# Joining the two token parts behind one stationary weight tile in the column products of a four-layer trunk

## Chip, core and metric

The kernel runs on one core of a Trainium2 chip. The metric is the device time of one execution in microseconds (us). Before the change three runs gave 1311.87 to 1312.33 us, with a median of 1312.16 us. Engines are named as in the profile: PE is the matrix engine (PEld is its loading of stationary operands), DVE the vector engine, ACT the scalar engine, POOL the general one, SP the one that issues most DMAs.

## What is computed

A trunk of four layers over 256 tokens of width 1024. Each layer has a mixer (differential attention, a gated recurrence called hgrn2, windowed attention called swa, differential attention again), a feed-forward network and a gate. Cut to its frame, the reference is:

```python
for i in range(DEPTH):
    y = (diff_attention, hgrn2, swa_sink_attention)[i % 3](h, ...)
    h = layer_norm(ALPHA * h + y, ln_g[i, 0], ln_b[i, 0])
    u = jnp.square(jax.nn.relu(h @ w_up[i])) @ w_down[i]      # 1024 -> 4096 -> 1024
    h = layer_norm(ALPHA * h + u, ln_g[i, 1], ln_b[i, 1])
    h = h + jax.nn.sigmoid(h @ w_ple_gate[i]) * (p[i] @ w_ple[i])
```

All of it is float32. The matrix products with weights are the bulk of the work.

## The kernel before

**Split products.** Each float32 operand of a product with weights is split into a high and a low float32r part: ACT copies the high part, DVE subtracts it from the source (`split`, L116 and L117). A product is then three matmuls, high with high, high with low, low with high, into one accumulator (`mm3`, L169 to L171). The weights of the whole trunk are packed on the host into chunks of 128 x 2048 numbers, read in the order of use (`read_w`), three raw buffers deep, and split into tiles `wh` and `wl`, of which four chunks are held.

**Two forms.** In the token-major form (`tokmm`) the tokens are stationary and 512 columns of weights move. In the column form (`colmm`, called by `col2`) a 128 x 128 tile of weights is stationary and 256 tokens move, so that the result comes out with its columns on the partitions. `col2` computes two such column tiles, `c` = 0 and 1, into the two halves of one PSUM bank: for each, eight k-tiles of 128 rows, three matmuls each. Then it calls `done(bank)`. The tokens' two parts are the tiles `hTh` and `hTl`, 128 x 8 x 256 each.

**Where the column form is used.** One chunk for each call of `col2`: 55 chunks of the up projection (`up` in `ffn`), 16 for query and key of the heads in the two differential attentions (`qk_gen`), 8 for query and forget gate in hgrn2 (`qf_gen`), 5 for key, value and query in swa (`kv_done`, `q_gen`). That is 84 chunks and 84 x 16 = 1344 pairs of a column tile and a k-tile, so 4032 matmuls of 256 columns. The `done` functions empty the bank: a Relu on ACT in `up` (L418) and a square on DVE (L419), copies on ACT in the attentions (L607, L611, L782), a sigmoid on ACT and two DVE operations in hgrn2 (L965 to L969).

**Order.** Dense products are generators in one queue (`push`), and the mixers pull them between the steps of their own work with `fill(us)`: each step of a generator yields an estimate of its time, 0.325 for a k-tile of `colmm`. In the feed-forward network the up product of chunk j + 1 comes ahead of the down product of chunk j, which accumulates in four banks called `acc`; the column form and all others use four banks called `mm`. ACT and DVE keep the order that the scheduler gave them and work on splits of later weights between the evictions.

Of the kernel before, what the change touches and what calls it, by code (L numbers as in the profile page):

```python
# [16 lines left out]
P = 128  # L17
D = 1024
S = 256
# [13 lines left out]
# chunks of weights that may be split ahead of earlier work on the scalar engine, and of  # L33
# softmax and relu work on the vector engine
# [7 lines left out]
def backward(ap):  # L42
    """The same view with its last dimension read from the end."""
    dims = [list(d) for d in ap.ap]
    step, n = dims[-1]
    dims[-1] = [-step, n]
    return bass.AP(ap.tensor, ap.offset + (n - 1) * step, dims)


class Weights:  # L50
    """A chunk of weights, split into two float32r parts, in halves of HC columns."""
# [4 lines left out]
    def sl(self, o, n):  # L56
        h, r = o // HC, o % HC
        return [t[h][:, r : r + n] for t in self.tiles]


class Trunk:
# [58 lines left out]
    # the engine's later splits of weights stay behind what it has been given so far  # L120
# [63 lines left out]
    def colmm(self, out, hT, w, col, width):  # L184
        for kt in range(KT):
            self.mm3(
                out, w.sl(kt * width + col, P), [x[:, kt, :] for x in hT], kt == 0, kt == KT - 1
            )
            yield 0.325

    # two column tiles of 128 into the halves of one bank, then done(bank)
    def col2(self, hT, done):
        w = self.load_w()
        ps = self.mm_ps()
        for c in range(2):
            yield from self.colmm(ps[:, c * S : c * S + S], hT, w, c * P, 256)
        done(ps)

    # token-major projection to 512 columns (4 k-tiles a chunk), then evac(blk, bank)
# [17 lines left out]
    # part c of a 1024 -> 1024 projection of one block (2 k-tiles a chunk)  # L217
# [6 lines left out]
    def new_hT(self):  # L224
        return [
            self.hp.tile([P, KT, S], F32R, name=self.nm(t), tag=t, bufs=2)
            for t in ("hTh", "hTl")
        ]

    def load_x(self, blk, k, pool):  # L230
        # four k-tiles of the transposed input
        xr = pool.tile([P, 4, P], F32, name=self.nm("qk"), tag="qk", bufs=3)
        self.nc.sync.dma_start(xr, self.ins["xT"][blk][:, k : k + 4])
        sl = slice(blk * P, blk * P + P)
        self.split(self.hT[0][:, k : k + 4, sl], self.hT[1][:, k : k + 4, sl], xr)

    def setup(self):
        nc, cp = self.nc, self.cp
        self.hT = self.new_hT()
        # keep the tensor engine busy while the first loads are under way: its clock is  # L240
        # gated to half when idle
        z = self.sp.tile([P, 512], BF16, name="z", tag="z", bufs=1)
# [9 lines left out]
    def bias_rows(self, pool):  # L252
        nc, cp, ins = self.nc, self.cp, self.ins
        # relative position biases, one row per head, by distance
# [26 lines left out]
    def load_bias(self, bt, a, lo, hi):  # L281
        d = self.ud[a]
        # row p holds query 127 - p of a block: the distance falls along the row
        src = bass.AP(d.tensor, d.offset + lo * UL, [[1, P], [UL, hi - lo], [1, 256]])
        self.nc.sync.dma_start(bt[:, lo:hi], src)
# [8 lines left out]
    def rpow(self, out, var, scale, eps):  # L294
        # out = (var * scale + eps) ** -0.5
# [45 lines left out]
    def out_part(self, c, blk):  # L341
        # k-tiles 2c, 2c + 1
# [11 lines left out]
    def out_end(self, i, later):  # L354
        # what is left of block 0, of block 1, then the work that needs neither
# [20 lines left out]
    # per-layer embedding, a generator for each block  # L376
# [26 lines left out]
    def ffn(self, i, last):  # L403
# [3 lines left out]
        with tc.tile_pool(name=f"fp{i}", bufs=4) as fp:  # L407
# [16 lines left out]
            # first chunks token-major, so that block 0 needn't wait for block 1  # L424
# [25 lines left out]
            def up(j):  # L450
                def done(ps):
                    r = relu2(ps, 512)
                    new_u(j)
                    self.split(us[j][0], us[j][1], r.rearrange("p (k t) -> p k t", k=2))

                yield from self.col2(hT, done)

# [58 lines left out]
            # gated per-layer embedding  # L516
# [30 lines left out]
    # the transposes of block 1 come when the next mixer has started on block 0  # L547
# [4 lines left out]
    def diff_attention(self, i):  # L552
# [5 lines left out]
        with tc.tile_pool(name=f"ap{i}", bufs=2) as ap:  # L558
# [45 lines left out]
            def qk_gen(hd):  # L604
                def done(ps):
                    qk = ap.tile([P, 2, S], F32, name=self.nm("qk"), tag="qk", bufs=3)
                    nc.scalar.copy(  # L607
                        qk[:, 0, :].rearrange("p (b t) -> p b t", b=2),
                        backward(ps[:, :S].rearrange("p (b t) -> p b t", b=2)),
                    )  # L610
                    nc.scalar.copy(qk[:, 1, :], ps[:, S:])  # L611
                    qks[hd] = qk
# [141 lines left out]
    def swa(self, i):  # L754
# [3 lines left out]
        with tc.tile_pool(name=f"ap{i}", bufs=2) as ap:  # L758
# [8 lines left out]
            def kv_done(ps):  # L767
                nc.scalar.copy(kv.rearrange("p a t -> p (a t)"), ps)
# [10 lines left out]
            def q_gen(c):  # L779
                def done(ps):  # L780
                    q = ap.tile([P, 2, S], F32, name=self.nm("q"), tag="q", bufs=3)
                    nc.scalar.copy(  # L782
                        q.rearrange("p a (b t) -> p (a b) t", b=2),
                        backward(ps.rearrange("p (n t) -> p n t", n=4)),
                    )
                    for n in range(2):
                        qs[2 * c + n] = q[:, n, :]
# [3 lines left out]
            def soft(a):  # L791
                # heads a (partitions 0..63) and a + 8 (partitions 64..127)
# [100 lines left out]
    def hgrn2(self, i):  # L893
        nc, tc, ins = self.nc, self.tc, self.ins
        with tc.tile_pool(name=f"ap{i}", bufs=2) as ap:
# [12 lines left out]
            # lower bound: softmax over depth, sum of rows 1..i  # L908
# [48 lines left out]
            def qf_gen(pr):  # L957
                qt[pr] = ap.tile([P, 2, S], F32, name=self.nm("hq"), tag="hq")
                Ft[pr] = ap.tile([P, 2, S], F32, name=self.nm("f"), tag="f")
                for a in range(2):  # L960
                    hd = 2 * pr + a

                    def done(ps):
                        sig = ap.tile([P, 512], F32, name=self.nm("sig"), tag="sig")
                        nc.scalar.activation(sig, ps, AF.Sigmoid)  # L965
                        nc.vector.tensor_tensor(
                            qt[pr][:, a, :], sig[:, :S], ps[:, :S], op=ALU.mult
                        )
                        nc.vector.tensor_scalar(  # L969
                            Ft[pr][:, a, :], sig[:, S:], ol[:, hd : hd + 1], lb[:, hd : hd + 1],  # L970
                            op0=ALU.mult, op1=ALU.add,
                        )
# [7 lines left out]
            def decay(pr):  # L980
                q, QP, KS, f = qt.pop(pr), Qt.pop(pr), Kt.pop(pr), Ft.pop(pr)
                # diagonal of the transposed decay products, zeros beside it
# [14 lines left out]
                for lv, h in enumerate(LEVELS):  # L997
                    # the first halves of level 32 and 64 are runs of rows: nothing beside them
# [146 lines left out]
def _cols(w, cols):  # L1145
    # [1024, n] -> [128, 8 * 256], k-tile major, of the given 256 columns
# [3 lines left out]
def _half(w):  # L1150
    # [1024, 512] -> two chunks of 4 k-tiles
# [4 lines left out]
def _rows(w):  # L1156
    # [n * 256, 1024] -> n chunks of 2 k-tiles
# [21 lines left out]
def pack(inputs, depth=DEPTH):  # L1179
# [38 lines left out]
    # distances by position in the reversed bias row: rel = 255 - position  # L1218
# [51 lines left out]
```

## Time and profile before

| what | value |
|---|---|
| median of three runs | 1312.16 us |
| the profiled execution's span, first to last instruction | 1310.3 us |
| median less span | 1.9 us |
| PE busy | 1303.0 us, 8378 matmuls |
| DVE busy | 874.1 us |
| ACT busy | 676.0 us |
| DMA | 240.26 MB, mean 183 GB/s |

The page gives the busy time of each engine and the chain of work that ended last. A busy time of PE counts overlapping matmuls once and does not say at which rate they follow each other; for that the starts of consecutive matmuls are read from the time line. Windows of the trace tell how full DVE is in a given stage.

### The profile page before, as it was taken

To read this page: it belongs to the slowest core of one execution; us is meant where nothing else is said; L and a number is where in the kernel's file an instruction comes from. 1 tells how busy PE (TensorE), PEld (TensorE's weight loads), DVE (VectorE), ACT (ScalarE), POOL (GpSimd) and SP (SyncE) were. 2 spreads that over 40 slices of the span, in tenths; PEclk is the share of its full clock that TensorE was granted. 3 is DMA by queue.
4 is the path that set the end of the run, shared out by engine and by line. 5 is a ranking of instruction groups with operands and counts; after the bars stand their busy time and mean duration, and the time that the engine had idled before them with its cause. 6 is when DMAs were issued, how large, how long until landed. Compare 5 with 4: busy or idle time off the path is not lost.

```text
span 1310.3 us, 21010 instructions
## 1 busy us (share of the span) xinstructions
PE 1303.0 (99%) x8378; PEld 1161.2 (89%) x8378; DVE 874.1 (67%) x1573; ACT 676.0 (52%) x1212; POOL 33.7 (3%) x44
## 2 busy tenths in 40 slices
PE   8999999999999999999999999999999999999998
PEld 6988999998899889999989888999989989999987
DVE  5877655557878876555577796555577777655556
ACT  4875544443743454444437755444446775444433
POOL 0001000000000010000000000000000000000000
PEclk9999999999999999999999999999999999999999
DMA  7845655453742356545547145554538344655540
GB/s 268 316 142 193 226 193 188 179 184 132 261 156 103 105 189 227 176 181 191 193 164 266 62 172 213 206 184 190 193 129 295 130 169 161 239 182 190 194 161 33
DMA packets 43091, 240.26 MB, mean 183 GB/s; under 512 B 4512, under 2 KB 11744, under 8 KB 16496
## 3 DMA queue, kind: packets, MB, share of 16 engines
q1 hardware_dynamic: 42992, 238.91, 50.3%
q8 instruction: 66, 1.08, 0.3%
q14 instruction: 33, 0.27, 0.1%
HBM read 237.79 MB, written 1.10 MB: 182 GB/s over the span
## 4 chain that ended last, share of the span: by engine, by line
PE 98%; DMA 1%; ACT 0%; DVE 0%; SPq 0%; issue 0%
PE mm L169 21%; PE mm L171 21%; PE mm L170 20%; PE acc L171 9%; PE acc L170 9%; PE acc L169 9%; PE acc L1010 2%; PE mm L309 1%; DMA wr<-in_w_dram 1%; PE mm L664 1%; PE acc L628 1%; PE acc L624 1%; DMA qk<-in_xT_dram 0%; PE acc L841 0%; PE mm L441 0%; PE acc L852 0%
## 5 line engine op out<-in xcount | busy, mean ns | idle before, releaser
L117 DVE TENSOR_TENSOR wl<-wr,wh 128x1024 fp32r<-128x1024 f32 (+1 forms) x548 | 511.6, 967 | 248.4 <-ACT wh L116 247.9
L116 ACT ACTIVATE wh<-wr 128x1024 fp32r<-128x1024 f32 (+1 forms) x548 | 443.7, 852 | 366.1 <-issue 141.8
L169 PE MATMUL mm<-hTh,wh 128*128 128x256 f32 x1344 | 384.5, 286 | 0.0
L171 PE MATMUL mm<-hTh,wl 128*128 128x256 f32 x1344 | 380.2, 283 | 0.2 <-DVE wl L117 0.2
L170 PE MATMUL mm<-hTl,wh 128*128 128x256 f32 x1344 | 380.1, 283 | 0.0
L169 PEld LDWEIGHTS mm<-hTh,wh 128*128 128x128 f32 x1344 | 257.0, 191 | 4.4 <-issue 1.8
L170 PEld LDWEIGHTS mm<-hTl,wh 128*128 128x128 f32 x1344 | 257.1, 191 | 2.4
L171 PEld LDWEIGHTS mm<-hTh,wl 128*128 128x128 f32 x1344 | 257.0, 191 | 0.5 <-DVE wl L117 0.4
L169 PE MATMUL acc<-wh,uh 128*128 128x512 f32 x512 | 202.2, 395 | 0.0
L171 PE MATMUL acc<-wh,ul 128*128 128x512 f32 x512 | 202.0, 395 | 0.0
L170 PE MATMUL acc<-wl,uh 128*128 128x512 f32 x512 | 201.8, 394 | 0.0
L169 PE MATMUL mm<-wh,hTh 128*128 128x512 f32 (+1 forms) x536 | 197.2, 368 | 1.4 <-ACT hTh L116 0.7
L170 PE MATMUL mm<-wl,hTh 128*128 128x512 f32 (+1 forms) x536 | 192.8, 360 | 0.5 <-DVE wl L117 0.5
L171 PE MATMUL mm<-wh,hTl 128*128 128x512 f32 (+1 forms) x536 | 192.6, 359 | 0.0
L171 PEld LDWEIGHTS acc<-wh,ul 128*128 128x128 f32 x512 | 96.4, 188 | 22.8
L169 PEld LDWEIGHTS mm<-wh,hTh 128*128 128x128 f32 x536 | 101.4, 189 | 16.2 <-ACT wh L116 1.5
L171 PEld LDWEIGHTS mm<-wh,hTl 128*128 128x128 f32 x536 | 101.2, 189 | 16.0 <-issue 1.0
L170 PEld LDWEIGHTS mm<-wl,hTh 128*128 128x128 f32 x536 | 101.4, 189 | 14.7 <-DVE wl L117 1.5
L169 PEld LDWEIGHTS acc<-wh,uh 128*128 128x128 f32 x512 | 96.7, 189 | 19.9
L170 PEld LDWEIGHTS acc<-wl,uh 128*128 128x128 f32 x512 | 96.5, 188 | 20.0
L116 ACT ACTIVATE uh<-r 128x512 fp32r<-128x512 f32 x55 | 34.8, 632 | 77.0 <-DVE r L419 77.0
L300 POOL TENSOR_TENSOR rs<-rp,mhalf 128x2 f32<-128x2 f32 (+2 forms) x36 | 31.3, 870 | 1234.1 <-DVE rp L299 1234.1
(164 smaller groups left out, 1002.3 us busy)
## 6 DMA issues: line engine op xcount, KB each, us to landing
wr<-in_w_dram SPq DMA_DIRECT2D x207, 1024.0 KB, 4.8
lng<-in_ln_g_dram SPq DMA_DIRECT2D x8, 512.0 KB, 3.8
lnb<-in_ln_b_dram SPq DMA_DIRECT2D x8, 512.0 KB, 4.9
bt<-ud SPq DMA_DIRECT2D x2, 2048.0 KB, 9.9
wr<-in_w_dram SPq DMA_DIRECT2D x8, 256.0 KB, 5.6
bt<-ud SPq DMA_DIRECT2D x1, 1280.0 KB, 14.4
qk<-in_xT_dram SPq DMA_DIRECT2D x4, 256.0 KB, 6.0
h<-in_x_dram SPq DMA_DIRECT2D x2, 512.0 KB, 12.5
```

The costliest lines, as they stand in the source:

```text
L116: self.nc.scalar.activation(hi, src, AF.Copy),
L117: self.nc.vector.tensor_tensor(lo, src, hi.bitcast(F32), op=ALU.subtract),
L169: mm(out, l[0], r[0], start=start, stop=False)
L170: mm(out, l[0], r[1], start=False, stop=False)
L171: mm(out, l[1], r[0], start=False, stop=stop)
L300: nc.gpsimd.tensor_tensor(out, t, self.mhalf[:, :n], op=ALU.pow)
L309: nc.tensor.transpose(pt[:, j * P : j * P + P], src[:, c : c + P], self.ident)
L624: nc.tensor.matmul(sc[:, 0:P], qk[r, 0, 0:P], qk[r, 1, 0:P], start=True, stop=True)
L628: nc.tensor.matmul(sc[:, P:384], qk[r, 0, P:S], qk[r, 1, :], start=True, stop=True)
L664: nc.tensor.transpose(pt[:, s], e[:, 0, s], self.ident)
L1010: nc.tensor.matmul(pl[lo:hi, o : o + w], KS[:, a, b * P + lo : b * P + hi], Qr[:, a, n0 : n0 + g, 1, :], start=True, stop=True,)
```

## The change

The tokens' two parts become one tile of 128 x 8 x 2 x 256, `both`, whose views are the old high and low parts. `colmm` now gives each column tile a whole bank. For each k-tile the high weights meet the 512 columns of both parts in one matmul, and the low weights meet the high part in a second matmul of 256 columns, which adds to the bank's upper half. The two halves are added when the bank is emptied (`join`): ACT copies the upper half to a small tile `cr`, DVE adds the lower half to it. `done` is called for each column tile, not for the two together. The Relu of `up` moves to DVE: one operation computes max(r, 0) times r. hgrn2's sigmoids work on the joined tiles of 256 columns. The estimate of a k-tile becomes 0.35.

```diff
+class Tokens(list):
+    def __init__(self, both):
+        super().__init__([both[:, :, 0, :], both[:, :, 1, :]])
+        self.both = both
...
-    def colmm(self, out, hT, w, col, width):
+    def colmm(self, bank, hT, w, col, width):
+        mm = self.nc.tensor.matmul
         for kt in range(KT):
-            self.mm3(
-                out, w.sl(kt * width + col, P), [x[:, kt, :] for x in hT], kt == 0, kt == KT - 1
-            )
-            yield 0.325
+            wh, wl = w.sl(kt * width + col, P)
+            mm(bank, wh, hT.both[:, kt].rearrange("p a t -> p (a t)"), start=kt == 0, stop=False)
+            mm(bank[:, S:], wl, hT[0][:, kt, :], start=False, stop=kt == KT - 1)
+            yield 0.35
+
+    def join(self, out, bank, rev=False):
+        x = self.wp.tile([P, S], F32, name=self.nm("cr"), tag="cr", bufs=2)
+        self.nc.scalar.copy(x, bank[:, S:])
+        views = [y.rearrange("p (b t) -> p b t", b=2) for y in (out, bank[:, :S], x)]
+        if rev:
+            views[1:] = [backward(y) for y in views[1:]]
+        self.nc.vector.tensor_tensor(*views, op=ALU.add)
...
     def col2(self, hT, done):
         w = self.load_w()
-        ps = self.mm_ps()
         for c in range(2):
-            yield from self.colmm(ps[:, c * S : c * S + S], hT, w, c * P, 256)
-        done(ps)
+            ps = self.mm_ps()
+            yield from self.colmm(ps, hT, w, c * P, 256)
+            done(c, ps)
...
             def up(j):
-                def done(ps):
-                    r = relu2(ps, 512)
-                    new_u(j)
-                    self.split(us[j][0], us[j][1], r.rearrange("p (k t) -> p k t", k=2))
+                r = fp.tile([P, 512], F32, name=self.nm("r"), tag="r", bufs=2)
+
+                def done(c, ps):
+                    self.join(r[:, c * S : c * S + S], ps)
 
                 yield from self.col2(hT, done)
+                nc.vector.scalar_tensor_tensor(r, r, 0.0, r, op0=ALU.max, op1=ALU.mult)
+                new_u(j)
+                self.split(us[j][0], us[j][1], r.rearrange("p (k t) -> p k t", k=2))
...
             def qk_gen(hd):
-                def done(ps):
-                    qk = ap.tile([P, 2, S], F32, name=self.nm("qk"), tag="qk", bufs=3)
-                    nc.scalar.copy(
-                        qk[:, 0, :].rearrange("p (b t) -> p b t", b=2),
-                        backward(ps[:, :S].rearrange("p (b t) -> p b t", b=2)),
-                    )
-                    nc.scalar.copy(qk[:, 1, :], ps[:, S:])
-                    qks[hd] = qk
+                def done(c, ps):
+                    if c == 0:
+                        qks[hd] = ap.tile([P, 2, S], F32, name=self.nm("qk"), tag="qk", bufs=3)
+                    self.join(qks[hd][:, c, :], ps, c == 0)
...
-                    def done(ps):
-                        sig = ap.tile([P, 512], F32, name=self.nm("sig"), tag="sig")
-                        nc.scalar.activation(sig, ps, AF.Sigmoid)
-                        nc.vector.tensor_tensor(
-                            qt[pr][:, a, :], sig[:, :S], ps[:, :S], op=ALU.mult
-                        )
-                        nc.vector.tensor_scalar(
-                            Ft[pr][:, a, :], sig[:, S:], ol[:, hd : hd + 1], lb[:, hd : hd + 1],
-                            op0=ALU.mult, op1=ALU.add,
-                        )
+                    def done(c, ps):
+                        x = ap.tile([P, S], F32, name=self.nm("sig"), tag="sig", bufs=3)
+                        self.join(x, ps)
+                        if c == 0:
+                            y = ap.tile([P, S], F32, name=self.nm("sig"), tag="sig", bufs=3)
+                            nc.scalar.activation(y, x, AF.Sigmoid)
+                            nc.vector.tensor_tensor(qt[pr][:, a, :], x, y, op=ALU.mult)
+                        else:
+                            nc.scalar.activation(x, x, AF.Sigmoid)
+                            nc.vector.tensor_scalar(
+                                Ft[pr][:, a, :], x, ol[:, hd : hd + 1], lb[:, hd : hd + 1],
+                                op0=ALU.mult, op1=ALU.add,
+                            )
```

PE in an up product, first column tile, two k-tiles, before (`mm_...` is the bank, `hTh` and `hTl` the token parts, the last name the stationary weights):

```order
L169 MATMUL mm_2720<-hTh_1374,wh_2712 128x256
L170 MATMUL mm_2720<-hTl_1375,wh_2712 128x256
L171 MATMUL mm_2720<-hTh_1374,wl_2713 128x256
L169 MATMUL mm_2720<-hTh_1374,wh_2716 128x256
L170 MATMUL mm_2720<-hTl_1375,wh_2716 128x256
L171 MATMUL mm_2720<-hTh_1374,wl_2717 128x256
```

and now, the end of a first column tile and the start of the second, which has a bank of its own:

```order
L197 MATMUL mm_2080<-hT_1284,wh_2076 128x512
L198 MATMUL mm_2080<-hT_1284,wl_2077 128x256
L197 MATMUL mm_2100<-hT_1284,wh_2072 128x512
L198 MATMUL mm_2100<-hT_1284,wl_2073 128x256
L197 MATMUL mm_2100<-hT_1284,wh_2072 128x512
L198 MATMUL mm_2100<-hT_1284,wl_2073 128x256
```

Three matmuls of a k-tile became two, with the same 768 columns. DVE in the feed-forward network, from one square to the next, before (`r` is the eviction's tile, `ul` the low part of its split, `wl` the low parts of later weights):

```order
L419 TENSOR_TENSOR r_2469<-r_2469 128x512
L117 TENSOR_TENSOR ul_2473<-r_2469,uh_2472 128x512
L117 TENSOR_TENSOR wl_2679<-wr_2676,wh_2678 128x1024
L117 TENSOR_TENSOR wl_2683<-wr_2676,wh_2682 128x1024
L117 TENSOR_TENSOR wl_2713<-wr_2710,wh_2712 128x1024
L117 TENSOR_TENSOR wl_2717<-wr_2710,wh_2716 128x1024
```

and now:

```order
L125 TENSOR_TENSOR wl_2218<-wr_2215,wh_2217 128x1024
L125 TENSOR_TENSOR wl_2222<-wr_2215,wh_2221 128x1024
L208 TENSOR_TENSOR r_2069<-mm_2080,cr_2097 128x256
L125 TENSOR_TENSOR wl_2253<-wr_2250,wh_2252 128x1024
L125 TENSOR_TENSOR wl_2257<-wr_2250,wh_2256 128x1024
L208 TENSOR_TENSOR r_2069<-mm_2100,cr_2117 128x256
L475 SCALAR_TENSOR_TENSOR r_2069<-r_2069 128x512
L125 TENSOR_TENSOR ul_2122<-r_2069,uh_2121 128x512
```

Two additions of 256 columns are new; the first stands between the splits of two chunks of weights. DVE in hgrn2 ahead of the first pair's decay products, which read `hq` and `KS`, before:

```order
L966 TENSOR_TENSOR hq_3591<-sig_3723,mm_3674 128x256
L969 TENSOR_SCALAR f_3592<-sig_3723,ol_3460,lb_3459 128x256
L117 TENSOR_TENSOR wl_4055<-wr_4046,wh_4054 128x512
L977 TENSOR_SCALAR KS_3728<-f_3592 128x512
L978 TENSOR_TENSOR QP_3727<-hq_3591,f_3592 128x512
```

and now:

```order
L208 TENSOR_TENSOR sig_3451<-mm_3434,cr_3452 128x256
L982 TENSOR_TENSOR hq_3357<-sig_3451,sig_3455 128x256
L125 TENSOR_TENSOR wl_3785<-wr_3782,wh_3784 128x512 x2
L125 TENSOR_TENSOR wl_3791<-wr_3782,wh_3790 128x512
L208 TENSOR_TENSOR sig_3475<-mm_3458,cr_3476 128x256
L125 TENSOR_TENSOR wl_3791<-wr_3782,wh_3790 128x512
L985 TENSOR_SCALAR f_3358<-sig_3475,ol_3227,lb_3226 128x256
L993 TENSOR_SCALAR KS_3482<-f_3358 128x512
```

`KS` now stands behind an addition, a split and the forget gate `f`, whose sigmoid ACT computes after that addition.

## Rows read from the trace of the kernel before

**Rows 1.** The page: PE's busy time, granted clock in 40 slices, chain that ended last.

```profile
PE 1303.0 (99%) x8378; PEld 1161.2 (89%) x8378; DVE 874.1 (67%) x1573; ACT 676.0 (52%) x1212; POOL 33.7 (3%) x44
...
PEclk9999999999999999999999999999999999999999
...
PE 98%; DMA 1%; ACT 0%; DVE 0%; SPq 0%; issue 0%
```

**Rows 2.** PE's waits: waiter, releaser, us in total, times, longest; five in all.

```profile
PE acc L246 <- DVE z L243: 1.2, 1, 1.2
...
PE mm L171 <- DVE wl L117: 0.2, 1, 0.2
```

**Rows 3.** Groups by form: count, busy us, mean ns of one; L170, L171 alike.

```profile
L169 PE MATMUL mm<-hTh,wh 128*128 128x256 f32 x1344 | 384.5, 286 | 0.0
```

**Rows 4.** Time line of PE, an up product: start us, duration us, line; 14 steps apart.

```profile
212.31 0.28 PE L169 MATMUL mm<-hTh,wh 128*128 128x256 f32 x1
...
213.99 0.28 PE L171 MATMUL mm<-hTh,wl 128*128 128x256 f32 x1
```

**Rows 5.** Time line of PE in the first layer's gate: 14 steps apart.

```profile
319.19 0.39 PE L171 MATMUL mm<-wh,hTl 128*128 128x512 f32 x1
...
322.37 0.39 PE L170 MATMUL mm<-wl,hTh 128*128 128x512 f32 x1
```

**Rows 6.** Time line of PE: a down product's first and last matmul, then up.

```profile
205.66 0.39 PE L169 MATMUL acc<-wh,uh 128*128 128x512 f32 x1
...
211.00 0.40 PE L171 MATMUL acc<-wh,ul 128*128 128x512 f32 x1
211.24 0.28 PE L169 MATMUL mm<-hTh,wh 128*128 128x256 f32 x1
211.36 0.28 PE L170 MATMUL mm<-hTl,wh 128*128 128x256 f32 x1
```

**Rows 7.** Time line of PE in mixers: after 512 columns 256; after 256, 512.

```profile
354.53 0.28 PE L169 MATMUL mm<-hTh,wh 128*128 128x256 f32 x1
354.64 0.28 PE L170 MATMUL mm<-hTl,wh 128*128 128x256 f32 x1
...
1054.58 0.40 PE L169 MATMUL mm<-wh,hTh 128*128 128x512 f32 x1
1054.82 0.40 PE L170 MATMUL mm<-wl,hTh 128*128 128x512 f32 x1
```

**Rows 8.** Groups by form: evictions and operations like the new ones.

```profile
L418 ACT ACTIVATE r<-mm 128x512 f32<-128x512 f32 x55 | 31.9, 580 | 9.1 <-PE mm L171 9.1
L328 DVE SCALAR_TENSOR_TENSOR h<-h,mv,lng 128x512 f32<-128x512 f32 x32 | 22.5, 745 | 0.0
L117 DVE TENSOR_TENSOR hTl<-acc,hTh 128x256 fp32r<-128x256 f32 x24 | 10.0, 419 | 1.1 <-ACT hTh L116 0.9
L611 ACT COPY qk<-mm 128x256 f32<-128x256 f32 x16 | 5.9, 367 | 0.0
```

**Rows 9.** Windows: length, busy us of PE, PEld, DVE, ACT, POOL; clock; DMA; GB/s.

```profile
27.00:92.00 65.00, 64.91 (x500) 58.81 (x501) 50.67 (x170) 50.56 (x155) 2.82 (x4) 1.00 0.67 249
140.00:300.00 160.00, 160.00 (x1008) 144.47 (x1007) 91.28 (x93) 72.04 (x84) 0.00 (x0) 1.00 0.54 198
365.00:470.00 105.00, 105.00 (x813) 96.37 (x812) 88.37 (x215) 42.33 (x101) 4.42 (x4) 1.00 0.33 122
370.00:387.00 17.00, 17.00 (x161) 16.62 (x159) 15.30 (x41) 5.58 (x10) 0.00 (x0) 1.00 0.32 122
```

**Rows 10.** Time lines of DVE and PE in hgrn2, ahead of the first decay.

```profile
368.65 0.42 DVE L977 TENSOR_SCALAR KS<-f 128x512 f32<-128x512 f32 x1
...
370.00 0.39 PE L989 MATMUL acc<-hq,KS 128*128 128x128 f32 x2
```

**Rows 11.** Time lines of ACT and PE in the first attention, a head's scores.

```profile
36.08 0.37 ACT L611 COPY qk<-mm 128x256 f32<-128x256 f32 x1
...
37.44 0.38 PE L624 MATMUL acc<-qk 64*128 64x128 f32 x2
```

More of the change, by code (lines that the diff above doesn't have):

```diff
@@ L224, in new_hT @@
     def new_hT(self):
[L225 to L228, printed above, removed]
+        t = self.hp.tile([P, KT, 2, S], F32R, name=self.nm("hT"), tag="hT", bufs=2)
+        return Tokens(t)
     def load_x(self, blk, k, pool):
@@ L239, in setup @@
         self.hT = self.new_hT()
-        z = self.sp.tile([P, 512], BF16, name="z", tag="z", bufs=1)
+        z = self.wp.tile([P, 512], BF16, name="z", tag="cr", bufs=2)
         nc.vector.memset(z, 0.0)
@@ L765, in swa, with kv_done @@
             v = ap.tile([P, 2, P], F32, name=self.nm("v"), tag="v", bufs=1)
-            def kv_done(ps):
-                nc.scalar.copy(kv.rearrange("p a t -> p (a t)"), ps)
+            def kv_done(c, ps):
+                self.join(kv[:, c, :], ps)
             kvg = self.push(self.col2(hT, kv_done))
@@ L779, in q_gen, with done @@
             def q_gen(c):
-                def done(ps):
[L781 to L784, printed above, removed]
-                    )
-                    for n in range(2):
-                        qs[2 * c + n] = q[:, n, :]
+                def done(n, ps):
+                    q = ap.tile([P, S], F32, name=self.nm("q"), tag="q", bufs=6)
+                    self.join(q, ps, True)
+                    qs[2 * c + n] = q
                 return self.push(self.col2(hT, done))
@@ L961, in qf_gen @@
                     hd = 2 * pr + a
-                    def done(ps):
-                        sig = ap.tile([P, 512], F32, name=self.nm("sig"), tag="sig")
-                        nc.scalar.activation(sig, ps, AF.Sigmoid)
-                        nc.vector.tensor_tensor(
-                            qt[pr][:, a, :], sig[:, :S], ps[:, :S], op=ALU.mult
-                        )
-                        nc.vector.tensor_scalar(
-                            Ft[pr][:, a, :], sig[:, S:], ol[:, hd : hd + 1], lb[:, hd : hd + 1],
-                            op0=ALU.mult, op1=ALU.add,
-                        )
+                    def done(c, ps):
[11 more added lines that the diff above has]
+                            )
                     yield from self.col2(hT, done)
```

## The prediction

> **What bounds the kernel now.** I read the page first. PE is busy for 1303.0 of 1310.3 us, the granted clock is at its upper level of 2.4 GHz in all 40 slices, and 98% of the chain that ended last is PE [rows 1]. Then the waits: five rows name PE as the waiter, the longest 1.2 us, the shortest 0.2 us, all at the start of the program [rows 2]. So nothing keeps PE waiting after the first microseconds. The time is the sum of the steps from one matmul's start to the next, and only what shortens these steps, or makes PE wait, shows.
>
> The column form has three groups of 1344 matmuls of 256 columns [rows 3]. The mean of one, 286 ns, is how long one stays in the pipeline, not its price. The price is the step between starts: in an up product 14 steps take 213.99 - 212.31 = 1.68 us, **120 ns** each [rows 4]. At 2.4 GHz 256 columns are 106.7 ns, so 13.3 ns go with the instruction. The kernel also has runs of 512 columns. In the gate 14 steps take 322.37 - 319.19 = 3.18 us, **227 ns** [rows 5], which is 213.3 + 13.7. The two agree: about 13.3 ns for each matmul with its own stationary tile, whatever its width. In the down products the step is longer: 23 steps from 205.66 to 211.00, 232 ns [rows 6].
>
> **PE's part of the change.** Columns stay the same (512 + 256 against 3 x 256), and one instruction of three goes. A pair of column tile and k-tile cost 3 x 120 = 360 ns; it will cost 227 + 120 = 347 ns if the 512 goes at the gate's step. 1344 x 13.3 ns = **17.9 us** less.
>
> No row shows the new mixture, 512 and 256 in turn, so I bound it by the changes of width that exist. Cheap end: the first 256 after a run of 512 steps in 354.64 - 354.53 = 0.11 us [rows 7], and with 227 the pair is 340 ns, 26.9 us less. Dear end: a down product's last 512 takes 0.24 us and the first 256 behind it 0.12 us (211.00, 211.24, 211.36) [rows 6]; read between the two rounded figures and the 360 of now that is about 357 ns, 4 us less. Going from 256 to 512, the first 512 takes 0.24 us [rows 7]: what is gained on one side of a change of width is given back on the other, 240 + 110 = 350. I stay at 347, nearest to the gate's row: the new matmuls write the same `mm` banks, and one operand is a weight tile and the other a token tile, as in the gate, while the 232 ns belong to the `acc` banks and the `u` tiles alone. An up product between two down products runs at 120, like those in the mixers, so it is not the stage that is slow.
>
> For a matmul's step the Trainium skill (TensorE: Matmul & The Clock Gate, section "Back-to-back issue gap") has columns over 2.4 plus 2.5 ns, for matmuls warm and alone. By it one matmul less in each pair is worth 1344 x 2.5 ns = 3.4 us, not 17.9. The rows don't agree with it: their excess is 13.3 ns for either width.
>
> **ACT and DVE.** In `up` ACT had one Relu of 580 ns and now has two copies of 367 ns: +0.15 us a chunk. DVE gains two additions, priced by the like subtraction from PSUM at 419 ns, and its square becomes a fused operation of 745 ns [rows 8]: about +0.9 us a chunk. In the network a chunk of up and one of down take 48 x 0.120 + 24 x 0.232 = 11.3 us, and DVE is busy 91.28 of 160 us there, 57% [rows 9]; 0.9 of 11.3 makes 65%. The cover is PE's own work on a chunk of down products ahead of the use. The first addition waits for half an up product, and two splits of a later chunk are queued behind it; those weights are wanted three or four chunks later, and their buffers come free only late in that same up product. So nothing there reaches PE: cost 0. If the cover were gone, it would be 55 x 0.9 = 50 us.
>
> In the mixers DVE is fuller: 50.67 of 65 us in the first attention, 88.37 of 105 in hgrn2, 15.30 of 17 in the first decay [rows 9]. Three places can make PE wait.
>
> *First decay of hgrn2.* `KS` was ready at 369.07 and used at 370.00, a slack of 0.93 us [rows 10]. The way from bank to `KS` was a sigmoid and DVE operations; now it is copy, addition, sigmoid, gate, `KS`: about 0.37 + 0.42 + 0.37 + 0.42 + 0.42 = 2.0 us and four changes of engine, each of which can find a split of up to 0.7 us at work. Estimate: between 0 and 1 us of wait, taken 0.5.
>
> *Decay products.* Four additions in the first decay are 4 x 0.34 to 0.42 us on 15.30, so about 16.8 us, in a stretch that PE would now pass in 17 - 28 x 0.0133 = 16.6. DVE becomes as long as PE. Splits of later weights can move out of the stretch, so the wait lies between 0 and 1 us, and the second decay is alike; taken 0.5 each.
>
> *Heads of the attentions.* The key copy ended at 36.45 and the scores started at 37.44: 0.99 us, the shortest slack of the 16 heads [rows 11]. The new tail has one copy less behind the last matmul and one addition more, with a hand-over: about +0.3 us, and at worst a split of 0.7 on top. Between 0 and 0.5 us a head, 0 to 8 in all; taken 1. In swa half of the queries are ready half a chunk earlier than before: 0.
>
> Sum of waits: 0.5 + 1 + 1 = 2.5 us, between 0 and about 11. On the profiled execution: 1310.3 - 17.9 + 2.5 = 1294.9 us; its span is 1.9 us under the median, so the **forecast is 1297 us**. DMA (54% busy in the network) need not go faster by more than 1%.
>
> **Rivals.**
> 1. *The dear step in the network.* The 880 up pairs cost 357 ns, since they stand between down products, and the 464 of the mixers 347: 2.6 + 6.2 - 2.5 = 6.3 us less, **1306**. For it: rows 6. Against: the 256s there settle at 120.
> 2. *A 512 behind a 256 stays dear.* Each new 512 stands behind a 256, and the one such step in the mixers took 0.24 us [rows 7], as a down product's last 512 did [rows 6]. Then the pair costs 240 + 120 = 360 ns as before, and the waits are left: 2.5 us more, **1315**, within 0.2%. Against: the steps of rows 5, and that a first 256 behind a 512 gives the same amount back. The skill's figure of 2.5 ns for each matmul leads to the same verdict by another way: 3.4 us less for PE, 2.5 more in waits, 1311.
> 3. *Slower: DVE becomes the bound of the mixers.* 29 chunks there bring 58 additions of 0.42 us, 24.4 us. If all of it came on PE's path, 24.4 - 17.9 = 6.5 us more, **1319**. It decides where DVE's idle time in a stage is less than its additions. Against: 14.3 us idle in the first attention for 16 additions of 6.7 us in all, 16.6 in hgrn2 [rows 9]. For: in-order queues, and the decays at 90%.
> 4. *The cheap step.* 340 ns a pair and 2.5 us of waits: **1288**. Against: the first 512 behind a 256 takes longer than 227 by about as much.
>
> That the change doesn't do what it says is not open: PE's order has 2688 matmuls for the 4032.
>
> **How the numbers follow.** A measurement of this kernel can tell about 0.2%, 2.6 us, from no change. Forecast (1291 to 1303) 0.58; rival 1 0.14; rival 2 0.10; rival 3 0.10; rival 4 0.08. Faster: 0.58 + 0.14 + 0.08 = 0.80. Same: 0.10. Slower: 0.10. The range leaves out rivals 2 and 3: 1287 to 1308.
>
> **What the profile after would show.** Starts of the new matmuls: 227 (512 to 256) and 120 (256 to 512), 347 a pair; 357 or more proves rival 1 or 2, by whether mixers and network differ. An up chunk of 16 pairs: 5.55 us against 5.76. PE's waits after the start: none in the network; waits on `KS`, `QP` and `qk` of some tenths in the mixers, 1 to 5 us in all; over 15 us is rival 3. DVE busy near 874 + 84 x 0.85 = 945 us. I am wrong if the pair steps in over 355 ns, or if PE waits in the network for `r`, `uh` or `wl`.

## The result and the profile after

The changed kernel takes 1302.76 us (median of 4 runs, 1302.48 to 1303.4), the kernel before 1312.06 us (4 runs on the same chip, 1311.87 to 1312.33): a ratio of **0.9931, 95% interval 0.9919 to 0.9943**, 9.3 us less. The forecast was 1297 us, 15 less: the sign and the mechanism are right, two fifths of the gain are missing.

The page after, the rows that answer to [rows 1]: span, busy times, granted clock, chain.

```profile
span 1300.8 us, 18541 instructions
...
PE 1293.9 (99%) x7034; PEld 1087.8 (84%) x7034; DVE 936.8 (72%) x1741; ACT 692.3 (53%) x1296; POOL 35.2 (3%) x44
...
PEclk9999999999999999999999999999999999999999
...
PE 98%; DMA 1%; ACT 0%; DVE 0%; issue 0%; SPq 0%
```

PE has 7034 matmuls for 8378, the clock is at its upper level throughout, and the chain is still PE. Its waits after, all of them, as [rows 2]:

```profile
PE acc L264 <- DVE z L261: 1.2, 1, 1.2
PE mm L177 <- ACT hT L124: 0.5, 1, 0.5
PE acc L177 <- ACT uh L124: 0.4, 1, 0.4
PE mm L177 <- ACT wh L124: 0.2, 1, 0.2
PE mm L178 <- DVE wl L125: 0.2, 1, 0.2
```

Nothing waits for `KS`, `qk` or an addition. One wait is new and stands in the network: 0.4 us on `uh` at the first down products of the third layer (793.61 us). So the difference is again a sum of steps. Adding up, from the trace, the time from each matmul's start to the next one's, by kind:

| kind | before, us | after, us | per pair or matmul, ns |
|---|---|---|---|
| column form, network (880 pairs) | 316.9 | 310.1 | pair 360.1 to 352.4 |
| column form, mixers (464 pairs) | 173.7 | 169.5 | pair 374.4 to 365.4 |
| down products (1536) | 357.3 | 358.0 | 232.6 to 233.1 |
| everything else | 462.4 | 463.1 | |

The column form gives 11.0 us where 17.9 were forecast; the rest gives back 1.4 where 2.5 were forecast; 1310.34 - 10.98 + 1.43 = 1300.79, the span after. The whole miss lies in one number: the pair. Time line of PE in an up product (start us, duration us), the answer to [rows 4, 7]:

```profile
208.90 0.39 PE L197 MATMUL mm<-hT,wh 128*128 128x512 f32 x1
209.12 0.28 PE L198 MATMUL mm<-hT,wl 128*128 128x256 f32 x1
209.24 0.40 PE L197 MATMUL mm<-hT,wh 128*128 128x512 f32 x1
209.47 0.28 PE L198 MATMUL mm<-hT,wl 128*128 128x256 f32 x1
209.59 0.40 PE L197 MATMUL mm<-hT,wh 128*128 128x512 f32 x1
209.83 0.28 PE L198 MATMUL mm<-hT,wl 128*128 128x256 f32 x1
209.94 0.40 PE L197 MATMUL mm<-hT,wh 128*128 128x512 f32 x1
```

The first pair, behind a down product, takes 0.34 us: 227 + 113 ns, rival 4's step. From the second on no pair of this chunk is cheap any more. In ns the steps go 232 + 118, 241 + 119, 236 + 114, and so on to the end of the chunk: three pairs in 1060 ns, then the same again.

45 of the 55 chunks of the network are like it, at 352.4 to 353.2 ns a pair, and the first chunk of each layer, which other matmuls interrupt, takes 356.1. Six are not: the second and third chunk of the first, second and fourth layer take 346.8 to 347.2 ns a pair, the sum that was forecast, in steps such as 230 + 116. Here are the start of one of the six and of the down product behind it, then the same of one of the 45:

```profile
153.03 0.39 PE L197 MATMUL mm<-hT,wh 128*128 128x512 f32 x1
...
158.58 0.39 PE L177 MATMUL acc<-wh,uh 128*128 128x512 f32 x1
...
197.69 0.39 PE L197 MATMUL mm<-hT,wh 128*128 128x512 f32 x1
...
203.33 0.39 PE L177 MATMUL acc<-wh,uh 128*128 128x512 f32 x1
```

A chunk of 16 pairs takes 5.55 us in the one and 5.64 in the other. By the program's allocation the two read the same weight buffers and the same token tile and write the same banks, in the same order. So neither the alternation of widths nor these addresses alone make a pair dear. Each second chunk of the six stands behind two chunks of down products in a row, but this alone doesn't do it either: in the run with doubled additions below, the two of the second layer take 353. What decides between 347 and 353 is not shown.

### The profile page after: what moved, and what is told of

The parts are those of the page before. It is cut to its first block, busy times and chain, and to the rows that moved or that the text cites. A ratio compares the mean times of both kernels' runs of the same rounds, so it can differ in the third digit from the quotient of the medians.

```text
span 1300.8 us, 18541 instructions
## 1 busy us (share of the span) xinstructions
PE 1293.9 (99%) x7034; PEld 1087.8 (84%) x7034; DVE 936.8 (72%) x1741; ACT 692.3 (53%) x1296; POOL 35.2 (3%) x44
## 4 chain that ended last, share of the span: by engine, by line
PE 98%; DMA 1%; ACT 0%; DVE 0%; issue 0%; SPq 0%
PE mm L197 24%; PE mm L198 12%; PE acc L177 9%; PE acc L179 9%; PE acc L178 9%; PE mm L177 9%; PE mm L179 9%; PE mm L178 8%; PE acc L1026 2%; PE mm L327 1%; DMA wr<-in_w_dram 1%; PE mm L681 1%; PE acc L645 1%; DMA qk<-in_xT_dram 1%; PE acc L641 1%; PE acc L854 0%
## 5 line engine op out<-in xcount | busy, mean ns | idle before, releaser
L197 PE MATMUL mm<-hT,wh 128*128 128x512 f32 x1344 | 480.9, 400 | 0.1
L198 PE MATMUL mm<-hT,wl 128*128 128x256 f32 x1344 | 377.4, 281 | 0.0
L197 PEld LDWEIGHTS mm<-hT,wh 128*128 128x128 f32 x1344 | 252.6, 188 | 60.1 <-issue 1.8
L198 PEld LDWEIGHTS mm<-hT,wl 128*128 128x128 f32 x1344 | 254.2, 189 | 3.0 <-DVE wl L125 0.4
L177 PE MATMUL mm<-wh,hT 128*128 128x512 f32 (+1 forms) x536 | 197.1, 368 | 0.8 <-ACT hT L124 0.5
L178 PE MATMUL mm<-wl,hT 128*128 128x512 f32 (+1 forms) x536 | 193.1, 360 | 0.4 <-DVE wl L125 0.2
L179 PE MATMUL mm<-wh,hT 128*128 128x512 f32 (+1 forms) x536 | 192.8, 360 | 0.0
L204 ACT COPY cr<-mm 128x256 f32<-128x256 f32 x168 | 61.1, 364 | 115.3 <-PE mm L198 115.2
L177 PEld LDWEIGHTS mm<-wh,hT 128*128 128x128 f32 x536 | 101.6, 190 | 16.2 <-ACT wh L124 1.6
L179 PEld LDWEIGHTS mm<-wh,hT 128*128 128x128 f32 x536 | 101.3, 189 | 15.8 <-issue 1.0
L178 PEld LDWEIGHTS mm<-wl,hT 128*128 128x128 f32 x536 | 101.5, 189 | 14.5 <-DVE wl L125 1.2
L208 DVE TENSOR_TENSOR r<-mm,cr 128x256 f32<-128x256 f32 x110 | 46.2, 420 | 28.5 <-ACT cr L204 23.2
```

The lines of the kernel that those rows point to most:

```text
L177: mm(out, l[0], r[0], start=start, stop=False)
L178: mm(out, l[0], r[1], start=False, stop=False)
L179: mm(out, l[1], r[0], start=False, stop=stop)
L197: mm(bank, wh, hT.both[:, kt].rearrange("p a t -> p (a t)"), start=kt == 0, stop=False)
L198: mm(bank[:, S:], wl, hT[0][:, kt, :], start=False, stop=kt == KT - 1)
L204: self.nc.scalar.copy(x, bank[:, S:])
```

## Experiments

Ratios are to the kernel before, with 95% intervals. "Network" is the up products, "mixers" the column products elsewhere.

**Each half alone.** In the first kernel only `up` uses the new form, the mixers keep `colmm` and their `done` functions of before; the second is the reverse.

```diff
-                yield from self.col2(hT, done)
+                yield from self.col2_old(hT, done)
```

> The new column form in the up projections alone (55 chunks, 880 pairs); the 29 chunks of the mixers keep the three matmuls of 256 columns and their old evictions. Theory, from the trace after: the pair steps at 353 ns in the network against 359.5 before, 880 x 6.7 = 5.9 us less than before, and the down products give 0.7 back: 1307 us. Rival: the mixers give nothing, since the joined evictions cost there what PE gains; then the whole 9.3 us stay: 1303. Second rival: the network gives nothing: 1312.

> The complement: the new column form in the mixers alone (29 chunks, 464 pairs), the up projections with three matmuls of 256 columns and the Relu on ACT. Theory: 464 pairs gain about 10 ns each, less some tenths of us of waits: 4 us less than before, 1308 us. Rival (mixers neutral): 1312. Second rival (mixers carry it all): 1303.

Network alone: 1305.75 us, ratio 0.9956 (0.9943 to 0.9968), where 1307 were expected. Mixers alone: 1308.81 us, 0.9977 (0.9968 to 0.9987), where 1308 were. The gains, 5.9 and 2.9 us, add up to 8.8 of 9.3, and the new pairs step in the network kernel as in the full one (235.6 + 116.8 ns). So the two halves are independent, neither spoils the other, and both fall short.

**The 512s alone.** The low-weight matmuls of the up products are left out (the low weights' part of u is missing).

```diff
-                yield from self.col2(hT, done)
+                yield from self.col2(hT, done, False)
```

> The up projections without the matmul of the low weights: it leaves that part of the product out. What is left there is an unbroken run of 512-column matmuls with the weights stationary. Theory A (turns are what costs): they step at 227 ns, as in the gate, and the time falls by 880 x (353 - 227) = 111 us to 1192. Rival B (the column form itself): they step at 232 to 236, 1196 to 1200. If DVE or DMA can't keep up with the shorter chunks, PE waits for wl or r show it.

One run: 1194.71 us, between the two theories' times, so the step has to tell them apart. Time line of PE, the 16 matmuls of an up product and the one behind them:

```profile
207.30 3.81 PE L197 MATMUL mm<-hT,wh 128*128 128x512 f32 x16
210.94 0.40 PE L177 MATMUL acc<-wh,uh 128*128 128x512 f32 x1
```

(210.94 - 207.30) / 16 = 228 ns, and from the fourth on 227. In a run the new 512 is no dearer than the gate's.

**Runs of one width.** The same matmuls, but a column tile issues its 8 high products, then its 8 low ones; then, in a second kernel, a chunk its 16 and 16, with two banks open.

```diff
             mm(bank, wh, hT.both[:, kt].rearrange("p a t -> p (a t)"), start=kt == 0, stop=False)
+            yield 0.23
+        for kt in range(KT):
+            wh, wl = w.sl(kt * width + col, P)
             mm(bank[:, S:], wl, hT[0][:, kt, :], start=False, stop=kt == KT - 1)
-            yield 0.35
+            yield 0.12
```

> The changed kernel with another order inside a column tile: first the eight matmuls of 512 columns, then the eight of 256, instead of in turn. Same instructions. Theory A: the pair is dear (353 instead of 347 ns) because the widths take turns; in runs of eight the 512 steps at 227 and the 256 at 113 to 120, 347 or less a pair: 1344 x 6 to 10 ns, 8 to 13 us less than the changed kernel, 1290 to 1295 us. Rival B: a 512 with weights stationary steps at 232 to 236 in the column form whatever stands beside it: within 2 us of the changed kernel, 1301 to 1305.

> Both column tiles of a chunk open at once: 16 matmuls of 512 columns, then 16 of 256, so that the width changes twice a chunk instead of 32 times (four times in e3_grouped). Theory: a change of width upsets the next four to six steps by 4 to 5 ns each, so longer runs win more: 228.3 + 119.8 = 348 ns a pair, against 349.7 in e3_grouped and 352.4 in turn; 1344 x 4.4 = 5.9 us less than the changed kernel, 1297 us. Rival: what is won on PE is lost in the evictions, which now come together at the end of a chunk: 1302 or more.

Runs of 8: 1302.03 us, 0.9926 (0.9912 to 0.9939); network pair 349.7 ns. Runs of 16: 1300.73 us, 0.9916 (0.9901 to 0.9931); pair 348.9. Inside a run the steps settle. The 256s go 113, 119, then 120. Behind a change from 256 to 512, at the second column tile in the runs of 8, the 512s go 234, 235, 229, 232, 231, then 227: five unsettled steps. At the start of a chunk there is no change of width, since the 512s of a down product stand ahead; there they go 236, 224, 231, 235, 229, 232, 231, then 227, in most chunks: seven. A run has to be longer than that to earn 227 + 120.

The time of the runs of 8 lies in the range of rival B, but their settled steps of 227 rule its reason out; the runs of 16 came out between the two expectations. The rest of the kernel lost much of what the network gained: with runs of 8, 1.9 of 2.4 us; with runs of 16 the up and down products gained 3.8 us and all else took 2.0 more. With runs of 16 a head's key is complete only at the end of the chunk, and this wait, absent above, shows in the waits of PE:

```profile
PE acc L640 <- DVE qk L199: 1.2, 3, 0.6
PE acc L690 <- ACT aT L682: 0.7, 1, 0.7
```

Runs of 16 in the network alone, then, with the mixers in turn:

```diff
-                yield from self.col2(hT, done)
+                yield from self.col2_runs(hT, done)
```

> The whole change, but in the network's up projections alone a chunk issues its 16 high products of 512 columns one after the other and then its 16 low ones of 256 columns; the mixers keep the two widths in turn. Theory (two widths in turn cost about 5 ns a pair more than runs of one width; the mixers lose from runs, since their column tiles end later): the network gains what the runs of 16 gained there when they were made everywhere (880 pairs, 3.1 us, and 0.7 us on the down products), the mixers stay as in the changed kernel: 1302.8 - 3.8 = 1299.0 us, pair 348.9 ns. Rival (the loss of the mixers in that run was chance, or came with the network's new order): 1300.7 us or above, with the mixers' steps longer than in the changed kernel.

1299.67 us, 0.9908 (0.9891 to 0.9925), against an expected 1299.0; the mixers' column products stay at 169.7 us (169.5 in the changed kernel), so the rival is out. One chunk on PE's time line:

```profile
198.00 3.82 PE L226 MATMUL mm<-hT,wh 128*128 128x512 f32 x16
201.66 2.08 PE L231 MATMUL mm<-hT,wl 128*128 128x256 f32 x16
203.57 0.39 PE L177 MATMUL acc<-wh,uh 128*128 128x512 f32 x1
```

3.66 / 16 = 229 ns and 1.91 / 16 = 119 ns: 5.57 us a chunk where most chunks of the changed kernel take 5.64.

**What the price of the additions is.** Each addition is done twice.

```diff
-        self.nc.vector.tensor_tensor(*views, op=ALU.add)
+        for _ in range(2):
+            self.nc.vector.tensor_tensor(*views, op=ALU.add)
```

> The changed kernel with each addition of the join done twice on DVE, with the same result: 168 more operations of 0.42 us, 46 us of them in the network and 24 us in the mixers. Theory: the evictions lie beside PE's work; the network takes it at no cost, the mixers at 0 to 3 us: 1303 to 1306. Rival: the additions stand on PE's path in the mixers, and the second costs what the first did: 10 to 24 us more, 1313 to 1327.

1307.28 us, 0.9969 (0.9958 to 0.9981): 4.5 us more than the changed kernel, above the theory's 3 and far below the rival's 13. DVE in the network and in hgrn2, the windows of [rows 9] (length; PE, PEld, DVE, ACT and POOL busy), with single additions first, doubled ones behind:

```profile
140.00:300.00 160.00, 160.00 (x794) 134.06 (x793) 104.47 (x125) 74.87 (x97) 0.98 (x1) 1.00 0.57 197
365.00:470.00 105.00, 104.88 (x708) 90.70 (x707) 91.34 (x225) 46.18 (x115) 5.25 (x4) 1.00 0.34 121
```

```profile
140.00:300.00 160.00, 160.00 (x797) 134.06 (x796) 115.96 (x153) 74.72 (x99) 0.93 (x1) 1.00 0.57 197
365.00:470.00 105.00, 104.17 (x705) 89.56 (x704) 92.09 (x235) 42.69 (x113) 4.78 (x4) 1.00 0.28 93
```

In the network DVE goes from 104.47 to 115.96 of 160 us and PE's steps there stay as they were to 0.2 us (the two chunks at 347 ns a pair in the second layer are now at 353): DVE is off the path with room to spare. The profiled span grew by 5.4 us, 0.7 of them in the mixers' column products and 4.6 outside the column and down products, where these waits are among the new ones:

```profile
PE mm L328 <- DVE h L352: 1.4, 1, 1.4
...
PE mm L682 <- DVE e L671: 0.9, 1, 0.9
...
PE acc L1006 <- DVE KS L994: 0.3, 1, 0.3
```

So the single additions still fit into the mixers' slack (PE's waits after name none of them), a second set does not.

**Why do 512 columns step at 232 in the down products?** The same question had been left at [rows 6]: these matmuls never settle, in runs of 24. Two first guesses, the PSUM bank and the place in SBUF:

```diff
-        pz = self.acc_ps()
+        pz = self.mm_ps()
```

```diff
-        self.wp = ec(tc.tile_pool(name="wp", bufs=1))
         self.hp = ec(tc.tile_pool(name="hp", bufs=1))
+        self.wp = ec(tc.tile_pool(name="wp", bufs=1))
```

> The changed kernel with the two sets of PSUM banks exchanged: the column products and the other mm tiles in banks 0 to 3, the down products in banks 4 to 7. Theory: which bank a matmul writes doesn't set its step; the pair stays at 353 ns in the network, the down products at 232, the gate at 227, time within 1.5 us of the changed kernel (1302.8). Rival: the longer steps belong to a set of banks; then the down products go to 227 (1536 x 5.6 ns, 8.6 us less) or the gate to 232.

> The changed kernel with the token tiles allocated below the weight tiles in SBUF instead of above; u tiles stay where they are, so that all distances between the stationary and the moving operand change. Theory: addresses don't set the step, all steps and the time as in the changed kernel within 1.5 us. Rival: they do; then the pair leaves 353 ns, or down 232, or the gate 227, and the time moves by 3 us or more.

1302.73 us (0.9931, 0.9917 to 0.9946) and 1302.99 us (0.9934, 0.9919 to 0.9948); down 233.1 ns in both, pair 352.4 and 352.2. The banks are out. The second run looked as if addresses were out too, which was wrong: by the program's allocation it had moved `hT` and the weights by multiples of 2048 bytes, and `u` not at all.

The next kernel edits the down products in four ways, one per layer.

```diff
-                nc.vector.scalar_tensor_tensor(r, r, 0.0, r, op0=ALU.max, op1=ALU.mult)
+                nc.vector.scalar_tensor_tensor(
+                    r, r, 1.0 if i == 0 else 0.0, r, op0=ALU.mult if i == 0 else ALU.max, op1=ALU.mult
+                )
...
-                    acc[blk][hf], us[j], (0, 1), blk, w,
-                    (hf * 512, 1024 + hf * 512), j == 0, j == NJ - 1,
+                    acc[blk][hf], hT if i == 1 else us[j], (0, 1), blk, w,
+                    (hf * 512, 1024 + hf * 512), j == 0 or i == 2, j == NJ - 1 or i == 2,
...
-            self.step = HC
+            self.step = 512 if i == 3 else HC
```

> One look at why the down products' 512-column steps stay at 232 to 233 ns where the gate's settle at 227. The whole change, with a different edit of the down products in each of the four layers, so that the output is not the reference's: layer 0 squares u without the relu (no zeros among the values that TensorE multiplies); in layer 1 the down products' stationary operand is taken from the normed input, which has been in SBUF long before, instead of from the u that VectorE has just written; in layer 2 each chunk's two k-tiles make an accumulation of their own (the earlier chunks' sums are dropped) instead of adding to sums of 64 k-tiles; in layer 3 the weight pieces of the network are split in halves of 512 instead of 1024 columns. If one of these properties sets the step, the down step is 227 ns in its layer and 232 to 233 in the other three. If none does, it is 232 to 233 in all four, and what is left is the place of the run behind an up projection and its length of 24.

One run, 1301.08 us. The mean down step by layer is 232.6, **228.0**, 234.6, 232.2 ns; the third layer has 234.6 in the changed kernel as well, where one step among its first down products takes 0.83 us. Time line of PE, the sixth and the last matmul of one run of 24, in layer 0 and in layer 1:

```profile
204.83 0.39 PE L179 MATMUL acc<-wh,ul 128*128 128x512 f32 x1
...
209.00 0.39 PE L179 MATMUL acc<-wh,ul 128*128 128x512 f32 x1
```

```profile
565.07 0.39 PE L179 MATMUL acc<-wh,hT 128*128 128x512 f32 x1
...
569.15 0.39 PE L179 MATMUL acc<-wh,hT 128*128 128x512 f32 x1
```

18 steps: 4.17 us (232 ns) and 4.08 us (227 ns). Moving operands, banks and order are the same; only the stationary tile differs. Zeros in u, the length of the accumulation and the width of the weights' splits are out. `hT` and `u` differ in three things: values, age, address. In the program's allocation the weights and `hT` begin, on every partition, at byte 224 of a block of 256, `u` at byte 96. One more run, with `hT` moved by 128 bytes in all layers and `u` layer by layer (in layer 2 u keeps its sign and is not squared, in layer 3 the down products take the u of the chunk before):

```diff
+        nc.gpsimd.memset(self.hp.tile([P, 32], F32, name="pad"), 0.0)
         self.hT = self.new_hT()
...
+            if i > 0:
+                nc.gpsimd.memset(fp.tile([P, 448 if i == 1 else 480], F32, name=self.nm("pd"), tag="pd", bufs=1), 0.0)
...
+                    r, r, 1.0 if i == 2 else 0.0, r, op0=ALU.mult if i == 2 else ALU.max,
+                    op1=ALU.max if i == 2 else ALU.mult,
...
-                    acc[blk][hf], us[j], (0, 1), blk, w,
+                    acc[blk][hf], us[max(j - 1, 0) if i == 3 else j], (0, 1), blk, w,
```

> One look. In the run before, the down products settled at 227 ns in the one layer whose stationary operand was the normed input. Three differences between that operand and u are told apart here: where it lies in SBUF (the normed input begins at the same byte offset within 256 as the weight pieces; u begins 128 bytes off), what values it has (both signs, u has none below zero), and how long ago it was written. The normed input is shifted by 128 bytes in all layers, and u's tiles are shifted layer by layer: layer 0, u at the weights' offset within 256 bytes; layer 1, u at the weights' offset within 2048 bytes; layers 2 and 3, u 128 bytes off as in the changed kernel. In layer 2 u is the up product itself, without relu and square, so that it has both signs; in layer 3 the down products take the u of the chunk before, which was written a chunk earlier (both change the output). Theory by address: the down step is 227 ns in layers 0 and 1 and 232 to 233 in layers 2 and 3, and the gate products, whose stationary operand is now 128 bytes off, go from 227 to about 232; the up pair may move from 352.4 either way, since its moving operand has moved against its stationary one. Theory by values: 227 in layer 2 alone. Theory by age: 227 in layer 3 alone. Under these two the gate stays at 227 and the up pair at 352.4.

One run, 1303.24 us. The mean down step by layer: **228.5, 228.8**, 234.9, 232.6 ns. Time line of PE, again the sixth and the last of 24, layer 0 and layer 2; behind them the fifth and the seventeenth matmul of the first layer's gate, which is [rows 5] with `hT` moved:

```profile
215.69 0.39 PE L179 MATMUL acc<-wh,ul 128*128 128x512 f32 x1
...
219.77 0.39 PE L179 MATMUL acc<-wh,ul 128*128 128x512 f32 x1
```

```profile
852.51 0.40 PE L179 MATMUL acc<-wh,ul 128*128 128x512 f32 x1
...
856.70 0.40 PE L179 MATMUL acc<-wh,ul 128*128 128x512 f32 x1
```

```profile
322.81 0.40 PE L178 MATMUL mm<-wl,hT 128*128 128x512 f32 x1
...
325.60 0.39 PE L178 MATMUL mm<-wl,hT 128*128 128x512 f32 x1
```

227 ns (4.08 / 18), 233 ns (4.19 / 18) and 232 ns (2.79 / 12). The down products became quick where u moved to byte 224, and the gate, quick before, became slow when its operand moved to byte 96. Both signs in layer 2 and a chunk more of age in layer 3 change nothing. The theory by address holds, on both sides. The up pair moved too, from 352.4 to 350.8 ns (231.0 + 119.8), with only its moving operand shifted, to 350.0 to 351.2 in all chunks but the first of each layer; none is at 347 there and none at 353. So addresses have a part in the price of the alternation, beside what is open above.

**Both findings together**: runs of 16 in the network, and u at byte 224.

```diff
             us = {}
+            pad = fp.tile([P, 32], F32, name=self.nm("pd"), tag="pd", bufs=1)
+            nc.gpsimd.memset(pad, 0.0)
```

> The kernel of the experiment with runs of 16 in the network, and u shifted by 128 bytes in every layer, so that it begins at the weights' offset within 256 bytes; nothing else moves, and the computation is whole. Theory by address: the down products' mean step goes from 232.7 ns to the 228.5 to 228.8 that the two shifted layers showed, 1536 times: 6.1 us less than the 1299.7 of the runs alone, 1293.6 us; gate and up steps as in that kernel (227; pair 348.9). Rival (the shifted normed input, not u, or a gain that another wait takes back): 1297 us or above.

**1290.85 us** (median of 5, 1290.46 to 1291.02), ratio **0.9835 (0.9821 to 0.9848)**: the best of all kernels here, 21 us under the kernel before and 12 under the changed one. One down product and the up product behind it:

```profile
203.46 0.39 PE L179 MATMUL acc<-wh,ul 128*128 128x512 f32 x1
...
207.54 0.39 PE L179 MATMUL acc<-wh,ul 128*128 128x512 f32 x1
207.77 0.62 PE L226 MATMUL mm<-hT,wh 128*128 128x512 f32 x2
```

(207.54 - 203.46) / 18 = 227 ns. Against the runs alone the down products lose 6.8 us, as expected (6.1), and the 512s of the up products another 1.4, which was not: behind a settled run of 512s the next run of 512s is settled from its first step (227.5 ns on the mean, for 229.1). Some 0.7 more lie outside both and are not explained.

## Why the prediction was right in sign and too large

- **What bounds the kernel.** Right: steps on PE, with waits of 3.3 us in all before and 2.5 after. The one new wait on `uh` (0.4 us) speaks against the "none in the network", and is small.
- **The pair, 347 ns: the step that failed.** It took the settled step of each width from a run of that width [rows 4, 5]. It measured 352.4 in the network (-7.7 of the hoped -13.3 ns) and 365.4 in the mixers (-9.0). The bounds of 340 and 357 held for the network. The rows in which the width changes gave 357 [rows 6] and "240 + 110 = 350" [rows 7], and I passed both over for a row in which it doesn't. At 350 in the network and the same 3 ns more in the mixers the forecast would have been about 1301 us (1344 x 3 ns = 4.0 us more). That would have been luck in part: 350 was a sum of two steps read to 10 ns, and no chunk of the network takes it. Most take 353, in steps between 232 and 242 and between 112 and 121, and six take the 347 of the forecast. So 347 can be had in turn, most chunks don't reach it, and why they don't stays open; the unsettled steps behind a single change of width, which the runs of 8 show, are no full answer, since the six have as many changes.
- **A chunk of up:** 5.55 us predicted; 5.64 measured in most, 5.55 in six.
- **"The 232 ns belong to the `acc` banks and the `u` tiles alone":** half right. Not the banks, the tiles: their address. The conclusion drawn from it, that the new matmuls are free of such a step, holds for a run of them and not in turn, where most have an unsettled step of their own.
- **ACT and DVE.** Right. Copy and addition take 364 and 420 ns (367 and 419 were taken), the fused square 691 (745):

```profile
L204 ACT COPY cr<-mm 128x256 f32<-128x256 f32 x168 | 61.1, 364 | 115.3 <-PE mm L198 115.2
L208 DVE TENSOR_TENSOR r<-mm,cr 128x256 f32<-128x256 f32 x110 | 46.2, 420 | 28.5 <-ACT cr L204 23.2
...
L475 DVE SCALAR_TENSOR_TENSOR r<-r 128x512 f32<-128x512 f32 x55 | 38.0, 691 | 1.7
```

  DVE in the network is at 104.47 of 160 us, 65% as forecast; over the span 936.8 us for about 945.
- **Waits, 2.5 us:** none of the three appeared as a wait; the steps of the other matmuls grew by 1.4 us in all. The first decay now begins at 366.57; from 366.5 to 383.5 DVE is at 14.93 of 17 us where 16.8 was feared, with 4 splits of weights for 6: two did move out, as the prediction allowed.
- **Rivals.** 1 (357 in the network) and 2 (360) are out by the time line, 4 (340) is true only of the first pair behind a down product, and not in every chunk; 3 is out by PE's waits after, and by the run with doubled additions: 168 more cost 4.5 us, next to none of it in the network.
- **The skill's gap.** By the formula of the Trainium skill (TensorE: Matmul & The Clock Gate, section "Back-to-back issue gap"), which is for a matmul alone, the pair would be (512 + 256) / 2.4 + 5 = 325 ns and the gain 3.4 us, both estimates. The trace agrees with neither: settled matmuls cost 13.3 ns over the columns each, and the column form gained 11.0 us.

## What to carry to other kernels

Price a new mixture of matmuls by a range from the rows in which the widths change, not from the settled runs of each width; and if widths must mix, put them in runs of 16 where the later end of a column tile has cover, which gained 3.1 us here. Read the steps of every chunk and not only the mean: two prices can hide in it. Look at the step of long runs: 232 where others take 227 is worth moving the stationary tile by 128 bytes, which gained 6.8 us here. An experiment that "moves" tiles tells only about the distances by which it moved them.

## What was not expected of the hardware

- A settled step is the columns at 2.4 GHz plus 13.3 ns at both widths (120 and 226.7 ns); unsettled ones follow a pattern, three pairs long in most chunks in turn (1060 ns), seven steps long in the down products (231, 232, 228, 230, 233, 241, 232).
- The same matmuls in the same order, on the same buffers, step at 347 ns a pair in one chunk and at 353 in another.
- In no long run did the 512s settle with the stationary operand at byte 96 of a block of 256 and the moving weights at byte 224 (down products, and the gate once moved there); with both at byte 224 they do, after five steps behind a change of width. Only these two offsets ran, and the weights never moved, so whether the offset counts by itself or against the moving operand is open, as is what makes the pattern, and what would keep the two widths at 347 in turn.
- Behind a run of 512s the state of that run carries over into the next: behind a settled one it starts at 225 to 228 ns, behind an unsettled one it needs seven steps in most chunks. Behind 256s a run of 512s starts unsettled (234, 236, 228, 232, 231, then 227 in the last kernel).
